# Where tiles begin in SBUF: fillers move the 256 column weight tile and the partial outputs' operands, and the branch statistics get one buffer

## The chip, the cores and the metric

The kernel runs on one core of a Trainium2 chip. The metric is the time of one execution on the device in microseconds (us), lower is better. A profiled execution and its trace come from the hardware profiler.

## The reference

One layer of a decoder trunk, sequence 2048, width 1024, all in float32:

```python
h = _rms_norm(x, pre_g)
proj = jnp.einsum('bsd,de->bse', h, w_in)            # 1024 -> 13 x 256 columns
aq, ak, av, ag, bu, bv, bg, cx, cg, dq, dk, dv, dg = jnp.split(proj, 13, axis=-1)
ya = _dilated_mixture(heads(aq), heads(ak), heads(av))   # 4 heads of 64, dilations 1, 4, 16
yb = _spatial_gating(bu, bv, sgu_g, sgu_w, sgu_b)
yc = _multiscale_pool(cx, pool_w, pool_scale)
yd = _retention(dq, dk, dv, ret_g)
y = jnp.concatenate([ya * silu(ag), yb * silu(bg), yc * silu(cg), yd * silu(dg)], axis=-1)
y = jnp.einsum('bse,ed->bsd', y, w_out)
out = x + _rms_norm(y, post_g)
```

`_dilated_mixture` runs three attention branches (dilations 4, 16, 1) per head and mixes their outputs by a softmax over their log-sum-exps.

## The kernel before, in words

**Precision.** Every large product is made of three float32r matmuls: an operand is split into a high and a low part (`hh` and `hl` for the normed input, `w[:, 0]` and `w[:, 1]` for weights, the two halves of a `yt` tile for outputs), and high times high, high times low and low times high are summed in PSUM. `mm(o, lhsT, rhs)` at L98 issues one: `lhsT` is the stationary operand, at most 128 columns, loaded into the array by a weight load (PEld) of its own; `rhs` is the moving operand, streamed through. A profile row names the output, then the moving and then the stationary operand: `ps_m<-w,hh` streams `w` through an array that holds a slice of `hh`.

**Stages.** First come the projections, in two halves of 1024 tokens. `prologue` loads x, norms it and transposes it (`ps_x`) into `hh` and `hl`. Slices of the weights are loaded and split by `weights`: 128 columns wide as `w128` or 256 wide as `w256`. Two shapes of product use them. `proj_t` (tile `ps_t`) holds 128 columns of `w128` stationary and streams 512 tokens of `hh` or `hl`. `proj_m` (tile `ps_m`) holds 128 tokens of `hh` or `hl` stationary and streams the 256 columns of `w256`; it makes `av`, `dv`, `dg` and `bv`. Results go to DRAM scratch, or feed the mixers B, C and D, which run among the projections.

Then comes attention, two pairs of heads (`attention(0)`, `attention(1)`), each head three branches: scores `ps_s`, softmax on VectorE (DVE) and ScalarE (ACT), transposes `ps_pt`, a split into `pt_hi` and `pt_lo`, and products `ps_o` with the stationary `att_v`. The first two branches of a head send their row statistics (minus the maximum, and the sum) through DRAM. The branch of dilation 1 writes its own into the third part of a tile `sv`, and `weigh` reads the others back into the first two parts and makes the mixing weights `wt`.

In the second pair's attention, nine `partial` outputs are spread: each loads a 128 token tile `yraw` of the mixers B, C and D, splits it into two `yt` tiles (`split_y`), multiplies them with `wo` (tile `ps_out`, `yt` stationary, 512 columns of `wo` moving, 36 matmuls) and stores the result `z` to `partd`. The tail, `final`, does the same for the other seven tiles, adds attention's part `ya` and `ysa`, the partial result, the norm and x (`xr`), and stores. Tile 9 of the tail takes its `yt` from the partials' buffers, the others from a pool of their own.

**Order.** A scheduler with a timeline of its own sets the order on each engine from the data dependences and the buffers; all DMAs go through SyncE's (SP) queue in its order. `tc.issue_after` ties each partial to a point of the attention.

**Places in SBUF.** Pools lie one behind the other, in order of opening, from low addresses up, and those with `side="right"` from the top down. In a pool, tiles lie in the order of their first use, a tag with n buffers taking n times its size. So a tile that is never written moves all that follow it by its size. Before, `align0` (384 bytes) and `align1` (32 twice) do that to bring the large tiles onto a multiple of 512 bytes. By these rules the tiles begin, in bytes past a multiple of 512 (before, then after where it differs):

| tile | use | before | after |
|---|---|---|---|
| `hh`, `hl` | moving in `ps_t`, stationary in `ps_m` | 0 | |
| `w128` | stationary in `ps_t` | 0 | |
| `w256` | moving in `ps_m` | 0 | 448 |
| `pt_hi`, `pt_lo` | moving in `ps_o` | 256 | |
| `att_v`, `q2`, `wo`, `ya0`, `ysa` of the tail | matmul operands | 0 | |
| `yt` of `partial` (and of tile 9) | stationary in `ps_out` | 480 | 0 |
| `yt` of the tail | stationary in `ps_out` | 0 | |
| `z`, `yraw`, `wo_raw`, `sga`, `wr`, `att_o` of the second pair | other engines, DMA, `wr` moving in `ps_f` | 480 | 0 |
| `sel` | stationary in `ps_f` | 32 | 64 |
| `sv` | statistics | 256 and 128 | 128, one place |

A slice of an operand within a tile starts at a multiple of 512 from the tile's start throughout (`w256`: 1024 bytes; a `yt` half: 512).

Of the kernel before, what the change touches and what calls it, by code (L numbers as in the profile page):

```python
# [9 lines left out]
F32 = mybir.dt.float32  # L10
# [8 lines left out]
P = 128  # L19
# [69 lines left out]
def hymba(ctx: ExitStack, tc: tile.TileContext, x, pre_g, w_in, sgu_g, sgu_w, sgu_b, pool_w,  # L89
# [4 lines left out]
    def r32(ap):  # L94
        return ap.bitcast(F32)
# [7 lines left out]
    cp = ctx.enter_context(tc.tile_pool(name="const", bufs=1))  # L103
# [15 lines left out]
    ya_d = [scratch(f"ya{g}", [P, 2, GRP]) for g in range(NG)]  # L119

    ident = cp.tile([P, P], F32, name="ident")
    cp.tile([P, 96], F32, name="align0")
    for _ in range(2):
        small.tile([P, 8], F32, tag="align1", name="align1")

# [22 lines left out]
    with ExitStack() as c1:  # L148
        k1 = c1.enter_context(tc.tile_pool(name="k1", bufs=1, side="right"))
        pa = c1.enter_context(tc.tile_pool(name="pa", bufs=1, reuse_waits="tile"))  # L150
# [40 lines left out]
        W2 = 6  # L191
        hT = {}
        first = []

        def prologue(gs, step):

# [43 lines left out]
        def weights(col, n, eng=V, scales=(1.0,)):  # L240

            if n == P:
                w = p1.tile([P, 2, KT, n], F32R, tag="w128", bufs=3, name="w128")
            else:
                w = pa.tile([P, 2, KT, n], F32R, tag="w256", bufs=1, name="w256")
            kc = KT * P // n
            for k in range(0, KT, kc):
                raw = p1.tile([P, kc, n], F32, tag="raw", bufs=2, name="raw")
                D.dma_start(raw, w_src[:, k:k + kc, col:col + n])
                for i, sc in enumerate(scales):  # L250
                    cs = slice(i * n // len(scales), (i + 1) * n // len(scales))
                    hi, lo = w[:, 0, k:k + kc, cs], w[:, 1, k:k + kc, cs]
                    A.activation(hi, raw[:, :, cs], AF.Copy, scale=sc)  # L253
                    if sc == 1.0:
                        eng.tensor_tensor(lo, raw[:, :, cs], r32(hi), ALU.subtract)  # L255
                    else:
                        V.scalar_tensor_tensor(lo, raw[:, :, cs], sc, r32(hi), ALU.mult, ALU.subtract)
            return w
# [285 lines left out]
    p3 = ctx.enter_context(tc.tile_pool(name="p3", bufs=1, side="right", reuse_waits="tile"))  # L544
# [15 lines left out]
    def attention(p, tab):  # L560
        o01 = (big if p == 0 else po).tile([P, 2, SEQ], F32, tag="big" if p == 0 else "o01", name="att_o01")
        o2 = po.tile([P, SEQ], F32, tag="o2", name="att_o2")
        o = [o01[:, 0], o01[:, 1], o2]
        wt = pc.tile([P, 3, 2, 2, 2, 8], F32, tag="wt", bufs=1, name="wt")
        for s in range(2):
            h = 2 * p + s
            rows = slice(s * HD, (s + 1) * HD)
            other = slice((1 - s) * HD, (2 - s) * HD)
            q2 = pm.tile([P, SEQ], F32R, tag="m8", bufs=7, name="q2")
            k2a = pm.tile([P, SEQ], F32R, tag="m8", bufs=7, name="k2a")  # L570
            k2b = pm.tile([P, SEQ], F32R, tag="m8", bufs=7, name="k2b")
            D.dma_start(r32(q2[rows]), qk_d[0][p][rows, 0])
            D.dma_start(r32(q2[other]), qk_d[0][p][rows, 1])
            for z in (rows, other):
                D.dma_start(r32(k2a[z]), qk_d[1][p][rows, 0])
                D.dma_start(r32(k2b[z]), qk_d[1][p][rows, 1])
            for b, dil in enumerate(DILS):
                vt = pm.tile([P, 16, 2 * HD], F32R, tag="m8", bufs=7, name="att_v")
                dst = r32(vt)
                if dil == 1:  # L580
                    src = v_d[h].rearrange("(n t c) d -> c t n d", c=4, t=32)
                    for c in range(4):
                        D.dma_start(dst[c * 32:(c + 1) * 32], src[c])
                elif dil == 4:
                    D.dma_start(dst.rearrange("q (j c) d -> q j (c d)", j=4),
                                v_d[h].rearrange("(j q c) d -> q j (c d)", j=4, c=4))
                else:
                    D.dma_start(dst.rearrange("q r d -> q (r d)"), v_d[h].rearrange("(q r) d -> q (r d)", r=16))
                qb = q2
                if dil != 1:  # L590
                    qb = pm.tile([P, SEQ], F32R, tag="m8", bufs=7, name="q2b")
                    if dil == 4:
                        src = r32(q2).rearrange("p (j k c i) -> p c j k i", j=4, c=4, i=8)
                        dst = qb.rearrange("p (j c k i) -> p c j k i", j=4, c=4, i=8)
                        for c in range(4):
                            (V if c < 3 else G).tensor_copy(dst[:, c], src[:, c])
                    else:
                        V.tensor_copy(qb.rearrange("p (r w i) -> p r w i", r=16, i=8),
                                      r32(q2).rearrange("p (w r i) -> p r w i", r=16, i=8))
                if dil == 1:  # L600
                    sv = p2.tile([P, 3, 2, 16], F32, tag="sv", bufs=2, name="sv")
                    raw = p2.tile([64, P], F32, tag="sT", bufs=1, name="sraw")
                    D.dma_start(raw, st_d[h].rearrange("b z (n q) -> (b z n) q", q=P))
                    branch(h, dil, qb, k2a, k2b, vt, tab, o[b], sv[:, b])
                    weigh(sv, raw, wt[:, :, :, s])
                    continue
                st = p2.tile([P, 2, 16], F32, tag="stat", bufs=2, name="att_st")
                branch(h, dil, qb, k2a, k2b, vt, tab, o[b], st)
                keep_stats(h, b, dil, st)
        return o01, o2, wt  # L610
# [136 lines left out]
    def weigh(sv, raw, w):  # L747

        pt = ps2.tile([P, GRP], F32, tag="t", bufs=N_T, name="ps_sv")
        transpose(pt[:, :64], raw, 64)  # L750
        V.tensor_copy(sv[:, :2].rearrange("q b z n -> q (b z n)"), pt[:, :64])
        nm = small.tile([P, 16], F32, tag="nm", name="nm")
        V.tensor_tensor(nm, sv[:, 0, 0], sv[:, 1, 0], ALU.min)
        V.tensor_tensor(nm, nm, sv[:, 2, 0], ALU.min)
        df = small.tile([P, 3, 16], F32, tag="df", name="df")
        V.tensor_tensor(df, sv[:, :, 0], nm.unsqueeze(1).broadcast_to([P, 3, 16]), ALU.subtract)
        ew = small.tile([P, 3, 16], F32, tag="ew", name="ew")
        A.activation(ew, df, AF.Exp, scale=-1.0)
        V.tensor_tensor(df, ew, sv[:, :, 1], ALU.mult)
        V.tensor_tensor(nm, df[:, 0], df[:, 1], ALU.add)  # L760
        V.tensor_tensor(nm, nm, df[:, 2], ALU.add)
        V.reciprocal(nm, nm)
        V.tensor_tensor(ew, ew, nm.unsqueeze(1).broadcast_to([P, 3, 16]), ALU.mult)
        eh = pc.tile([P, 3, 16], F32R, tag="eh", bufs=1, name="eh")
        V.tensor_copy(eh, ew)
        V.tensor_copy(w[:, :, :, 0], r32(eh).rearrange("q b (g n) -> q b g n", g=2))
        for b in range(3):
            V.tensor_tensor(w[:, b, :, 1], ew[:, b].rearrange("q (g n) -> q g n", g=2),
                            r32(eh[:, b]).rearrange("q (g n) -> q g n", g=2), ALU.subtract)
# [44 lines left out]
    def load_y(t, pool):  # L814
        raw = pool.tile([P, 6, P], F32, tag="yraw", bufs=2, name="yraw")
        D.dma_start(raw, yb_d[t // 4][:, t % 4])
        return raw

    def split_y(raw, pool, eng):

        ys = []
        for e in range(0, 6, 3):
            yt = pool.tile([P, 3, 2, P], F32R, tag="yt", bufs=2, name="yt")
            src = raw[:, e:e + 3]
            if eng is A:
                A.activation(yt[:, :, 0], src, AF.Copy)
            else:
                eng.tensor_copy(yt[:, :, 0], src)
            G.tensor_tensor(yt[:, :, 1], src, r32(yt[:, :, 0]), ALU.subtract)
            ys += [yt[:, j] for j in range(3)]  # L830
        return ys
# [12 lines left out]
    def partial(t):  # L844
        z = p3.tile([P, DM], F32, tag="z", bufs=2, name="z")
        ys = split_y(load_y(t, p3), p3, G)
        for n in range(2):
            A.activation(z[:, n * GRP:(n + 1) * GRP], out_proj(ys, range(2, 8), n, ps2, "part"), AF.Copy)
        D.dma_start(part_d[t * P:(t + 1) * P], z)
# [33 lines left out]
    with ExitStack() as c2:  # L883
        pm = c2.enter_context(tc.tile_pool(name="pm", bufs=1, reuse_waits="tile"))
        p2 = c2.enter_context(tc.tile_pool(name="p2", bufs=1, reuse_waits="tile"))
# [60 lines left out]
```

## Time and profile before

| | us |
|---|---|
| median of 3 runs | 1059.02 (1055.12 to 1059.49) |
| the profiled execution | 1055.14 |
| its span in the trace | 1053.4 |
| TensorE busy (PE) | 1000.1 |
| weight loads (PEld) | 861.6 |
| VectorE (DVE) | 519.1 |
| ScalarE (ACT) | 376.4 |
| GpSimd (POOL) | 228.0 |

Projections and mixers fill the span to about 640 us, attention 655 to 914, the tail the rest. A row of instructions gives start and length in us, engine, line, operation, tiles, shape, and how many equal ones follow each other; matmuls overlap, so a row of n lasts n - 1 steps from start to start and one full length. A row of a stretch gives the stretch, its length, and then for each engine busy time and, in brackets, how many instructions fell in it; asked for one tile, it counts that tile's instructions alone.

### The profile page before, as it was taken

Reading aid. Unit: us, or ns where it says so; the run is one execution under the profiler, and the core shown is the slowest. Engines: PE = TensorE matmul, PEld = TensorE weight load, DVE = VectorE, ACT = ScalarE, POOL = GpSimd, SP = SyncE. Lnnn points to the kernel's source line nnn. Section 1 sums busy time; section 2 is a strip of 40 time slices with the busy share of each in tenths; the row PEclk is TensorE's granted clock in tenths of the full one; section 3 lists DMA queues with packets and bytes.
Section 4 is the critical chain, followed back from the end, with each engine's and each line's share of the span. In section 5 each row is a group of like instructions: output and inputs, shape, how many; then the busy total and the mean of one; then the engine's idle time right before and its main releaser. Section 6 shows DMA issues by size and latency. Waiting matters only on the chain.

```text
span 1053.4 us, 15825 instructions
## 1 busy us (share of the span) xinstructions
PE 1000.1 (95%) x5960; PEld 861.6 (82%) x5960; DVE 519.1 (49%) x1584; ACT 376.4 (36%) x871; POOL 228.0 (22%) x217
## 2 busy tenths in 40 slices
PE   5899999999999999999999999988999989899994
PEld 5889898998888998989898888777896979776773
DVE  7621215687323331031666222176876667727776
ACT  6320313132212431031221111297873878612231
POOL 2310002221133000002120124031116411313444
PEclk9999999999999999999999999996999989989998
DMA  7530222332423232040310661187474663445565
GB/s 284 146 100 21 81 80 81 121 107 72 123 68 103 91 95 65 1 140 34 128 61 21 154 179 41 62 219 203 102 212 141 161 202 77 154 142 181 175 250 220
DMA packets 110988, 128.91 MB, mean 122 GB/s; under 512 B 9888, under 2 KB 88992, under 8 KB 108864
## 3 DMA queue, kind: packets, MB, share of 16 engines
q1 hardware_dynamic: 110912, 127.90, 39.7%
q8 instruction: 47, 0.77, 0.3%
q14 instruction: 29, 0.24, 0.1%
HBM read 91.57 MB, written 36.31 MB: 121 GB/s over the span
## 4 chain that ended last, share of the span: by engine, by line
PE 82%; DMA 7%; DVE 6%; ACT 2%; issue 2%; POOL 1%; SPq 1%; DVEq 0%; POOLq 0%; ACTq 0%
PE ps_t L98 38%; PE ps_m L98 16%; PE ps_out L98 10%; PE ps_s L98 4%; PE ps_o L98 4%; PE ps_pt L101 3%; PE ps_of L98 2%; DMA out_dram<-z 2%; DMA k2b<-qk 2%; DMA cm<-in_cmix_dram 1%; PE ps_in L98 1%; POOL z L877 1%; PE ps_mix L98 1%; DMA raw<-in_w_in_dram 1%; PE ps_x L101 1%
## 5 line engine op out<-in xcount | busy, mean ns | idle before, releaser
L98 PE MATMUL ps_t<-hh,w 128*128 128x512 f32 x1152 | 366.9, 395 | 0.0
L98 PEld LDWEIGHTS ps_t<-hh,w 128*128 128x128 f32 x1152 | 215.9, 188 | 47.8 <-issue 3.4
L98 PE MATMUL ps_t<-hl,w 128*128 128x512 f32 x576 | 226.1, 393 | 0.0
L98 PE MATMUL ps_m<-w,hh 128*128 128x256 f32 x1024 | 190.1, 286 | 1.6 <-ACT hh L235 1.6
L98 PEld LDWEIGHTS ps_m<-w,hh 128*128 128x128 f32 x1024 | 161.3, 193 | 3.3 <-ACT hh L235 2.2
L98 PE MATMUL ps_out<-wo,yt 128*128 128x512 f32 x576 | 153.9, 406 | 0.6 <-DVE z L875 0.6
L98 PE MATMUL ps_m<-w,hl 128*128 128x256 f32 x512 | 147.7, 288 | 0.1
L98 PEld LDWEIGHTS ps_t<-hl,w 128*128 128x128 f32 x576 | 108.3, 188 | 23.2 <-issue 1.4
L98 PEld LDWEIGHTS ps_out<-wo,yt 128*128 128x128 f32 x576 | 105.6, 192 | 23.1 <-issue 2.8
L255 DVE TENSOR_TENSOR w<-raw,w 128x1024 fp32r<-128x1024 f32 x42 | 58.5, 1402 | 109.5 <-ACT w L253 109.5
L98 PEld LDWEIGHTS ps_m<-w,hl 128*128 128x128 f32 x512 | 98.8, 193 | 0.8 <-DVE hl L236 0.3
L253 ACT ACTIVATE w<-raw 128x1024 fp32r<-128x1024 f32 (+1 forms) x56 | 55.0, 997 | 67.7 <-PE ps_t L98 37.3
L652 DVE CUSTOM_DVE_ANT_0 att_p<-ps_s,tab 128x128 f32<-128x128 f32 (+1 forms) x192 | 60.6, 360 | 36.3 <-PE ps_s L98 29.6
L662 DVE TENSOR_TENSOR pt_lo<-ps_pt,pt_hi 128x512 fp32r<-128x512 f32 x80 | 51.5, 652 | 18.6 <-ACT pt_hi L661 18.2
L654 ACT ACTIVATE att_p<-att_p,att_st 128x128 f32<-128x128 f32 (+1 forms) x128 | 55.0, 433 | 6.9 <-DVE att_st L652 6.4
L98 PE MATMUL ps_o<-pt_hi,att_v 128*128 128x128 f32 (+1 forms) x204 | 53.9, 284 | 1.7 <-DVE att_o L677 1.7
L98 PE MATMUL ps_o<-pt_lo,att_v 128*128 128x128 f32 (+1 forms) x204 | 52.9, 294 | 0.4 <-DVE pt_lo L662 0.4
L101 PE MATMUL ps_pt<-ident,att_p 128*128 128x128 f32 x300 | 50.6, 285 | 2.7 <-ACT att_p L654 2.5
L449 POOL TENSOR_TENSOR d_g<-d_g,ret_b 128x512 f32<-128x512 f32 x8 | 10.4, 1296 | 184.6 <-ACT d_g L447 184.6
L661 ACT ACTIVATE pt_hi<-ps_pt 128x512 fp32r<-128x512 f32 x80 | 44.1, 565 | 12.0 <-PE ps_pt L101 6.4
L98 PEld LDWEIGHTS ps_o<-pt_hi,att_v 128*128 128x128 f32 x204 | 41.0, 201 | 4.3 <-DVE att_o L677 1.9
L877 POOL TENSOR_TENSOR z<-z,xr 128x1024 f32<-128x1024 f32 x15 | 35.8, 2390 | 32.4 <-DVE z L875 27.7
(174 smaller groups left out, 1409.9 us busy)
## 6 DMA issues: line engine op xcount, KB each, us to landing
raw<-in_w_in_dram SPq DMA_DIRECT2D x52, 512.0 KB
qk<-qk_s SPq DMA_DIRECT2D x16, 512.0 KB
att_v<-vd SPq DMA_DIRECT2D x8, 1024.0 KB
xr<-in_x_dram SPq DMA_DIRECT2D x16, 512.0 KB
out_dram<-z SPq DMA_DIRECT2D x15, 512.0 KB
xt<-in_x_dram SPq DMA_DIRECT2D x7, 1024.0 KB
yraw<-yb SPq DMA_DIRECT2D x16, 384.0 KB
partd<-z SPq DMA_DIRECT2D x9, 512.0 KB
```

What stands on the lines that cost most here:

```text
L98: return T.matmul(o, lhsT, rhs, start=start, stop=stop, skip_group_check=True)
L101: T.transpose(o, i, ident[:n, :n])
L253: A.activation(hi, raw[:, :, cs], AF.Copy, scale=sc)
L255: eng.tensor_tensor(lo, raw[:, :, cs], r32(hi), ALU.subtract)
L449: G.tensor_tensor(o, o, ret_b.unsqueeze(1).broadcast_to([P, 2, 256]), ALU.mult)
L652: V.tensor_tensor_reduce(out=pr[:, u, :w], in0=ps[:, u, :w], in1=bb, scale=-SLOPES[h] * HD ** -0.5, scalar=3e38, op0=ALU.add, op1=ALU.min, ...
L654: A.activation(pr[:, u, :w], pr[:, u, :w], AF.Exp, bias=neg, scale=-1.0, accum_out=st[:, 1, n:n + 1])
L661: A.activation(hi, pt[:, :w], AF.Copy)
L662: V.tensor_tensor(lo, pt[:, :w], r32(hi), ALU.subtract)
L877: (V if last else G).tensor_tensor(z[:, ns], z[:, ns], xr[:, ns], ALU.add)
```

## The change

It adds three fillers and takes one away, and gives `sv` a single, permanent place.

- `sv` becomes `svs`, allocated once in the constants' pool where the filler `align0` stood, of the same 384 bytes; the two buffers of the tag `sv` in pool `p2` go, 768 bytes.
- In pool `pa`, ahead of the first `w256`, a filler of 448 bytes (`align2`) is laid, and behind it one of 64 (`align3`). Together 512, so all later tiles move by a whole 512.
- In pool `p3` at the top, behind the first `yt`, a filler of 480 bytes (`align4`) is laid. `p3` grows downwards, so all of `p3` and the pools opened after it on that side move 480 bytes down.

```diff
     ident = cp.tile([P, P], F32, name="ident")
-    cp.tile([P, 96], F32, name="align0")
+    svs = cp.tile([P, 3, 2, 16], F32, name="sv")
...
         first = []
+        align = []
...
             else:
+                if not align:
+                    align.append(pa.tile([P, 112], F32, name="align2"))
                 w = pa.tile([P, 2, KT, n], F32R, tag="w256", bufs=1, name="w256")
+                if len(align) == 1:
+                    align.append(pa.tile([P, 16], F32, name="align3"))
...
-                    sv = p2.tile([P, 3, 2, 16], F32, tag="sv", bufs=2, name="sv")
+                    sv = svs
...
         ys = split_y(load_y(t, p3), p3, G)
+        if t == 0:
+            p3.tile([P, 120], F32, name="align4")
```

No instruction is added or removed on any engine. The order is the same up to the last partial; in the tail the scheduler places some differently. On SP, at the end of the last partial: `ya` is attention's first pair, `partd<-z` the store of the last partial, `wo_raw` the last slice of the output weights, `xr` x for the residual, `yraw` a tile of the tail. Before:

```order
L910 DMA ya_8990<-ya_82 128x1024
L849 DMA partd<-z 128x1024
L553 DMA wo_raw<-in_w_out_dram 128x1024
L910 DMA ya_8991<-ya_83 128x1024
L911 DMA post_b<-in_post_g_dram 128x1024
L860 DMA xr<-in_x_dram 128x1024 x3
L816 DMA yraw<-yb_76 128x768
```

After:

```order
L917 DMA ya_8989<-ya_82 128x1024
L917 DMA ya_8990<-ya_83 128x1024
L918 DMA post_b<-in_post_g_dram 128x1024
L867 DMA xr<-in_x_dram 128x1024 x3
L821 DMA yraw<-yb_76 128x768
L856 DMA partd<-z 128x1024
L558 DMA wo_raw<-in_w_out_dram 128x1024
```

The store, which waits for the partial's result, and the load of `wo_raw` went behind six other loads. On PE, in the middle of the tail, where `ps_f` spreads the mixing weights of attention's second pair for VectorE and `ps_out` is the output product of the tiles. Before:

```order
L98 MATMUL ps_out<-wo_8965,ya_8990 128x512 x12
L98 MATMUL ps_f<-wr,sel 128x384 x5
L98 MATMUL ps_out<-wo_7117,yt 128x512 x6
L98 MATMUL ps_out<-wo_7126,yt 128x512 x6
L98 MATMUL ps_out<-wo_7135,yt 128x512 x6
L98 MATMUL ps_out<-wo_8965,ya_8993 128x512 x3
L98 MATMUL ps_out<-wo_8965,ysa 128x512 x3
L98 MATMUL ps_f<-wr,sel 128x384
```

After:

```order
L98 MATMUL ps_out<-wo_8964,ya_8989 128x512 x12
L98 MATMUL ps_f<-wr,sel 128x384 x6
L98 MATMUL ps_out<-wo_8964,ya_8989 128x512 x6
L98 MATMUL ps_out<-wo_8964,ysa 128x512 x12
L98 MATMUL ps_out<-wo_7117,yt 128x512 x6
L98 MATMUL ps_out<-wo_7126,yt 128x512 x5
L98 MATMUL ps_out<-wo_8964,ysa 128x512 x6
L98 MATMUL ps_out<-wo_7126,yt 128x512
```

The sixth `ps_f` no longer stands behind a whole tile of the output product, and attention's part of three partial tiles comes ahead of that tile.

## The prediction

> **What bounds the kernel now.** I read the page's busy shares and slices first, then the stretches stage by stage.
>
> ```profile
> span 1053.4 us, 15825 instructions
> PE 1000.1 (95%) x5960; PEld 861.6 (82%) x5960; DVE 519.1 (49%) x1584; ACT 376.4 (36%) x871; POOL 228.0 (22%) x217
> PEclk9999999999999999999999999996999989989998
> ```
>
> ```profile
> 0.00:50.00 50.00, 35.53 (x253) 33.07 (x254) 35.59 (x107) 26.12 (x41) 15.29 (x13) 1.00 0.69 227
> 345.00:380.00 35.00, 34.82 (x264) 33.10 (x263) 13.99 (x19) 13.97 (x21) 0.00 (x0) 1.00 0.30 91
> 450.00:640.00 190.00, 189.84 (x1190) 163.16 (x1189) 81.06 (x235) 36.73 (x50) 33.21 (x33) 1.00 0.35 103
> 680.00:760.00 80.00, 70.19 (x466) 63.19 (x466) 57.35 (x230) 68.86 (x219) 17.46 (x14) 0.89 0.67 168
> 760.00:860.00 100.00, 94.02 (x599) 81.53 (x596) 69.04 (x237) 67.34 (x202) 36.41 (x45) 0.97 0.65 186
> 960.00:1053.40 93.40, 74.97 (x320) 59.05 (x318) 66.14 (x215) 21.19 (x63) 41.79 (x23) 0.95 0.63 225
> ```
>
> The columns after each stretch's length are PE, PEld, DVE, ACT, POOL, the granted clock, the DMA share and GB/s. TensorE has no gap of note in the projection stages (189.84 of 190 us), at full clock. A nanosecond off each matmul there arrives at the end undiminished. In attention (680 to 860) PE is busy 164.2 of 180 us, 91%, and in the tail 75 of 93.4. A busy PE is not PE at its peak, so the question is how far apart matmuls start. For that I took stretches that hold one kind of matmul only, first `ps_m` (its moving operand is the 256 column weight tile), then `ps_t` (moving `hh` or `hl`, 512 columns).
>
> ```profile
> 95.00:115.00 20.00, 20.00 (x169) 20.00 (x169) 0.00 (x0) 1.79 (x3) 1.00 0.01 2
> ```
>
> ```profile
> 60.00:90.00 30.00, 30.00 (x134) 24.84 (x133) 2.08 (x3) 1.80 (x3) 1.00 0.25 71
> ```
>
> One record lasts 0.28 us in the first and 0.39 in the second, so a matmul starts each (20.00 + 0.28) / 169 = 120.0 ns and each (30.00 + 0.39) / 134 = 226.8 ns. The 256 columns more cost 106.8 ns, so streaming 256 columns takes 106.8 ns and each matmul, of either width, carries 13.2 ns beside it. All four operands of these two start on a multiple of 512 bytes. The change can win nothing but part of those 13.2 ns.
>
> **Part 1, the partial outputs' operands.** `yt` of `partial` starts 480 bytes past a multiple of 512; `yt` of most of `final` starts on one. Same instruction, same moving operand `wo`, 18 in a row, the first three rows from the partials and the last two from the tail:
>
> ```profile
> 787.74 4.36 PE L98 MATMUL ps_out<-wo,yt 128*128 128x512 f32 x18
> 801.44 4.47 PE L98 MATMUL ps_out<-wo,yt 128*128 128x512 f32 x18
> 913.92 4.42 PE L98 MATMUL ps_out<-wo,yt 128*128 128x512 f32 x18
> 993.43 4.24 PE L98 MATMUL ps_out<-wo,yt 128*128 128x512 f32 x18
> 1018.10 4.24 PE L98 MATMUL ps_out<-wo,yt 128*128 128x512 f32 x18
> ```
>
> The shift costs at least 4.36 - 4.24 = 0.12 us in 18, or 7.1 ns in each of the 17 steps; the two longer rows may hold a pause besides. The aligned rows step by (4.24 - 0.39) / 17 = 226.5 ns, as `ps_t` does. Nine partials issue 9 x 36 = 324 of these, 18 groups: 18 x 0.12 = 2.2 us. At attention's 91% that is 2.0 us, and tile 9 of the tail, which uses the same buffers, adds 2 groups or 0.2. I take -2.2 us, between 0 (if attention's waits swallow it) and 20 x 0.2 = -4.0 (if the longer rows hold no pause).
>
> The Trainium skill, "SBUF — State Buffer", section "Specifications (TRN2)", gives SBUF lines of 16 bytes, with a penalty for each cross to a new line. Both 480 and 448 are multiples of 16, so by that rule neither shift changes the lines crossed and both parts of the sum are zero, 1059.0 us. The rows above, 4.36 against 4.24 us, do not agree.
>
> **Part 2, the weight tile.** `w256` moves from a multiple of 512 to 448 past one. It is the moving operand of all `ps_m`:
>
> ```profile
> L98 PE MATMUL ps_m<-w,hh 128*128 128x256 f32 x1024 | 190.1, 286 | 1.6 <-ACT hh L235 1.6
> L98 PE MATMUL ps_m<-w,hl 128*128 128x256 f32 x512 | 147.7, 288 | 0.1
> ```
>
> That is 1536 matmuls. The same matmuls by stage:
>
> ```profile
> 0.00:50.00 50.00, 27.56 (x182) 24.37 (x182) 2.05 (x3) 1.79 (x3) 1.00 0.69 227
> 50.00:345.00 295.00, 72.72 (x586) 71.15 (x586) 0.69 (x1) 7.66 (x13) 1.00 0.28 86
> 345.00:380.00 35.00, 23.72 (x172) 21.55 (x173) 2.08 (x3) 1.79 (x3) 1.00 0.30 91
> 380.00:640.00 260.00, 73.87 (x598) 72.30 (x596) 0.69 (x1) 7.66 (x13) 1.00 0.30 88
> ```
>
> 586 + 598 = 1184 run where PE never waits and count in full. The other 352 run beside the transposes of x; from 0 to 50 PE idles 14.5 us, so I count half: 1184 + 176 = 1360.
>
> No row before has a moving operand 448 past a multiple. From below, the whole 13.2 ns beside the stream may go: -13.2 x 1360 = -18.0 us. From above, the step that `yt` pays may come to w256: +7.1 x 1360 = +9.7 us. The nearest row is the other 256 column matmul, `ps_o`, whose moving `pt_hi` and `pt_lo` start 256 past a multiple while its stationary `att_v` is on one:
>
> ```profile
> 846.63 0.28 PE L98 MATMUL ps_o<-pt_hi,att_v 128*128 128x256 f32 x1
> 846.74 0.28 PE L98 MATMUL ps_o<-pt_lo,att_v 128*128 128x256 f32 x1
> 846.86 0.28 PE L98 MATMUL ps_o<-pt_hi,att_v 128*128 128x256 f32 x1
> 846.98 0.28 PE L98 MATMUL ps_o<-pt_lo,att_v 128*128 128x256 f32 x1
> 847.10 0.28 PE L98 MATMUL ps_o<-pt_hi,att_v 128*128 128x256 f32 x1
> ```
>
> (847.10 - 846.63) / 4 = 117.5 ns: 2.5 ns better than 120.0, not worse. There is a second hint. `yt`'s 7.1 ns is about half of 13.2, as if the time beside the stream came in steps of that size, two now and three for `yt`. And the weight load shows it too:
>
> ```profile
> L98 PEld LDWEIGHTS ps_t<-hh,w 128*128 128x128 f32 x1152 | 215.9, 188 | 47.8 <-issue 3.4
> L98 PEld LDWEIGHTS ps_m<-w,hh 128*128 128x128 f32 x1024 | 161.3, 193 | 3.3 <-ACT hh L235 2.2
> ```
>
> Loads of the same size from operands that start on a multiple of 512 last 188 ns under `ps_t` and 193 under `ps_m`, so a load and a stream that start together seem to get in each other's way, and another start for the stream can end that. I take the middle between the nearest row's 2.5 ns and one step of 13.2 / 2 = 6.6: 4.5 ns, 4.5 x 1360 = -6.1 us.
>
> **Part 3, one buffer of statistics.** The next head writes `sv` only after the last read of the head before. The closest pair:
>
> ```profile
> 744.37 0.20 DVE L759 TENSOR_TENSOR df<-ew,sv 128x48 f32<-128x48 f32 x1
> 756.40 0.07 DVE L652 DVE_READ_ACCUMULATOR2_ANT sv<- 128x1 f32 x1
> ```
>
> 12 us lie between, so the new wait has ended before DVE comes to it: 0. Were this cover gone, DVE's next statistic would queue behind, and ACT's exponential waits for that.
>
> **Part 4, the tail's order.** Instructions are the same in number on every engine, and in the same order until the last partial. After that, SP issues the last partial's store and `wo_raw` behind the loads of `ya`, `post_b`, `xr` and `yraw`, and PE has six `ps_f` in one row. Nothing was measured in that order. PE's idle 18.4 us after 960 is the most a better order could win. Against it stands the longest wait there now, or the landing of `wo_raw` a few us later:
>
> ```profile
> PE ps_w L101 <- DVE wt L768: 5.4, 2, 4.2
> 1034.49 7.65 DMA out_dram<-z
> ```
>
> The tail's end is paced by stores and loads of 512 KB (the second row, from the chain, is 7.65 us of it), not by PE. I take 0, and -3 to +5 us for the range, since a single wait of the size shown is what an order typically moves.
>
> **Sum.** -2.2 - 6.1 + 0 + 0 = -8.3 us. The profiled execution took 1055.1 us (span 1053.4 and 1.7 around it) and would take 1046.8. It lies at the low end of the runs shown, whose median is 1059.0; on that median, 1050.7 us, 0.8% faster. About 0.5%, 5.3 us, is what a measurement can tell from no change.
>
> **The rivals.** First, the weight tile's place does nothing. For it: 117.5 comes from four short steps only, and 13.2 ns is the same under 256 and 512 columns, as a fixed cost of a matmul would be. Against: 193 against 188 ns for the load. Then -2.2 us, 1056.8, the same within 0.5%. The Trainium skill, "TensorE: Matmul & The Clock Gate", section "Step-by-step: what each phase is for", says the stationary and the moving operand come through two independent read ports; by that the place of one against the other is indifferent, and it is this rival's time. The trace leans against it, with 7.1 ns more where the stationary `yt` alone lies elsewhere, though `yt` may be slow by itself.
>
> Second, slower: any operand that crosses one more boundary of 512 bytes pays the `yt` step. Slices of `w256`, 1024 bytes each, touch three such stretches instead of two. Then +9.7 - 2.2 = +7.5 us, 1066.5. `ps_o` speaks against it, since `pt_hi` crosses as well and is not slower. It beats the gain of part 1 from +1.6 ns a matmul on, and is slower by 0.5% from +5.5 ns on.
>
> Third, all of the 13.2 ns goes: -18.0 - 2.2 = -20.2 us, 1038.8. No row shows a 256 column matmul at 107 ns.
>
> Fourth, the forecast holds up to 905 us and the tail's new order gives it back, +5 us: 1055.7, the same.
>
> **How the numbers follow.** Forecast 0.45 (2.5 to 6.6 ns give -5.6 to -11.2 us, 1048 to 1053.5, with the tail 1045 to 1056); nothing from the weight tile 0.27; slower by the step 0.12; all of it 0.10; lost in the tail 0.06. Faster: 0.45 + 0.10 = 0.55. Same: 0.27 + 0.06 = 0.33. Slower: 0.12. The range of 1041 to 1062 leaves out most of the third rival and of the second, near 2 in 10 together.
>
> **What would show it.** In the changed profile, a stretch of `ps_m` alone should hold about 20.28 / 0.1155 = 176 matmuls in 20 us instead of 169, and its loads should fall from 193 towards 188 ns. The partials' rows of 18 should read 4.24. `ps_t` should stay at 226.8, and the projections should end about 6 us earlier. The next write of `sv` should show no wait. I am wrong if `ps_m` stays at 120.0, if it rises towards 127, or if the attention starts earlier and the end does not.

## The result and the profile after

| | before | after |
|---|---|---|
| median, us | 1058.30 (1055.12 to 1059.49, 4 runs) | 1047.67 (1046.05 to 1048.31, 4 runs) |
| profiled execution, us | 1055.14 | 1046.05 |
| its span, us | 1053.4 | 1044.3 |

The changed kernel takes 0.9899 of the time before, 95% interval [0.9876, 0.9922]: 1.0% faster, against 0.8% forecast. In the pair of profiled executions, against which the sum was made, the gain is 9.1 us; forecast were 8.3.

The page after: span, busy time and, from its groups, the `ps_m` matmuls and their weight loads. The two numbers behind the bar are busy time in us and the mean length of one in ns.

```profile
span 1044.3 us, 15824 instructions
PE 994.1 (95%) x5960; PEld 856.4 (82%) x5960; DVE 520.7 (50%) x1584; ACT 376.7 (36%) x871; POOL 228.8 (22%) x217
L98 PE MATMUL ps_m<-w,hh 128*128 128x256 f32 x1024 | 184.8, 283 | 1.2 <-ACT hh L236 1.1
L98 PEld LDWEIGHTS ps_m<-w,hh 128*128 128x128 f32 x1024 | 158.1, 190 | 2.7 <-ACT hh L236 1.5
L98 PE MATMUL ps_m<-w,hl 128*128 128x256 f32 x512 | 145.8, 285 | 0.2 <-DVE hl L237 0.2
L98 PEld LDWEIGHTS ps_m<-w,hl 128*128 128x128 f32 x512 | 97.9, 191 | 0.8 <-DVE hl L237 0.4
```

TensorE's busy time fell by 6.0 us and that of its weight loads by 5.2; no other engine's moved by 2 us. The groups say where: `ps_m<-w,hh` lost 5.3 us, `ps_m<-w,hl` 1.9.

The stretches of the prediction again, counting `ps_m` and then `ps_t` alone. A second one of `ps_m` joins them, which held before:

```profile
141.00:161.00 20.00, 20.00 (x169) 20.00 (x169) 0.00 (x0) 1.79 (x3) 1.00 0.07 27
```

After, the two of `ps_m`, and the one of `ps_t`:

```profile
95.00:115.00 20.00, 20.00 (x172) 20.00 (x171) 0.00 (x0) 1.79 (x3) 1.00 0.00 1
141.00:161.00 20.00, 20.00 (x179) 20.00 (x178) 0.00 (x0) 1.80 (x3) 1.00 0.07 27
```

```profile
60.00:90.00 30.00, 30.00 (x134) 24.85 (x133) 2.08 (x3) 1.79 (x3) 1.00 0.24 71
```

`ps_t` holds 134 matmuls as before. `ps_m` no longer has one step: 20.28 / 172 = 117.9 ns in the first stretch and 20.28 / 179 = 113.3 in the second, where 120.0 stood in both. A step is the time from one matmul's start to the next one's. Behind the first few of a stage, single steps are 117 to 119 ns there and 113 to 114 ns, for a whole stage on end: two settled levels, not a spread.

To find where the 9.1 us lie, three points divide the span: the last `ps_t`, the start of the last partial's row of 18, and the issue of the last two loads of partial results on SP. In the timelines, before:

```profile
681.42 0.39 PE L98 MATMUL ps_t<-hh,w 128*128 128x512 f32 x1
1031.48 2.00 SPq L856 DMA_DIRECT2D z<-partd  x2
```

and after, with the partials' three rows of 18:

```profile
675.94 0.39 PE L98 MATMUL ps_t<-hh,w 128*128 128x512 f32 x1
781.61 4.27 PE L98 MATMUL ps_out<-wo,yt 128*128 128x512 f32 x18
795.21 4.37 PE L98 MATMUL ps_out<-wo,yt 128*128 128x512 f32 x18
907.67 4.32 PE L98 MATMUL ps_out<-wo,yt 128*128 128x512 f32 x18
1021.43 3.36 SPq L863 DMA_DIRECT2D z<-partd  x2
```

| stretch | before, us | after, us | difference |
|---|---|---|---|
| start to the last `ps_t` | 681.42 | 675.94 | -5.5 |
| from there to the last partial's row (before: 913.92) | 232.50 | 231.73 | -0.8 |
| from there to the last loads of `partd` | 117.56 | 113.76 | -3.8 |
| from there to the end | 21.92 | 22.87 | +0.9 |

So in this pair the projections gave 5.5 us, attention with its partials 0.8, and the tail about 2.9. The first is clear: the last `ps_t` starts at 680.6 to 682.3 us in all five traces of this study that leave `w256` on 0. The 0.8 us is not: the stretch from there to the last row takes 230.7 to 232.5 us in the five traces whose partials' `yt` stays at 480.

### The profile page after: what moved, and what is told of

Same layout as the page of the kernel before. It is cut to its first block, busy times and chain, and to the rows that moved or that the text cites. A ratio compares the mean times of both kernels' runs of the same rounds, so it can differ in the third digit from the quotient of the medians.

```text
span 1044.3 us, 15824 instructions
## 1 busy us (share of the span) xinstructions
PE 994.1 (95%) x5960; PEld 856.4 (82%) x5960; DVE 520.7 (50%) x1584; ACT 376.7 (36%) x871; POOL 228.8 (22%) x217
## 4 chain that ended last, share of the span: by engine, by line
PE 82%; DMA 8%; DVE 5%; POOL 2%; issue 1%; ACT 1%; SPq 1%; DVEq 0%; POOLq 0%; ACTq 0%
PE ps_t L98 38%; PE ps_m L98 15%; PE ps_out L98 11%; PE ps_o L98 4%; PE ps_s L98 3%; PE ps_pt L101 3%; PE ps_of L98 2%; DMA z<-partd 2%; DMA k2b<-qk 2%; DMA ret_b<-in_ret_g_dram 1%; PE ps_in L98 1%; DMA raw<-in_w_in_dram 1%; PE ps_mix L98 1%; DMA wo_raw<-in_w_out_dram 1%; DVE z L882 1%
## 5 line engine op out<-in xcount | busy, mean ns | idle before, releaser
L98 PE MATMUL ps_m<-w,hh 128*128 128x256 f32 x1024 | 184.8, 283 | 1.2 <-ACT hh L236 1.1
L98 PEld LDWEIGHTS ps_m<-w,hh 128*128 128x128 f32 x1024 | 158.1, 190 | 2.7 <-ACT hh L236 1.5
L834 POOL TENSOR_TENSOR yt<-yraw,yt 128x384 fp32r<-128x384 f32 x32 | 32.4, 1017 | 52.5 <-ACT yt L831 51.5
```

The lines of the kernel that those rows point to most:

```text
L98: return T.matmul(o, lhsT, rhs, start=start, stop=stop, skip_group_check=True)
```

## The experiments

**The weight tile alone.** The kernel before with the fillers around `w256` only:

```diff
+                if not align:
+                    align.append(pa.tile([P, 112], F32, name="align2"))
                 w = pa.tile([P, 2, KT, n], F32R, tag="w256", bufs=1, name="w256")
+                if len(align) == 1:
+                    align.append(pa.tile([P, 16], F32, name="align3"))
```

> The weight tile alone moves 448 bytes past a multiple of 512; the partials' yt stays at 480, sv keeps two buffers, and every engine has the order of the kernel before. If the shorter steps of ps_m carry the change (5.2 us less in the sum of steps of the changed trace), this run is 5 us faster than before, ratio about 0.995, with ps_m at 113 to 118 ns from start to start, rows of 18 ps_out of the partials still at 4.36 to 4.47 us, and about 13.8 us from the last matmul's start to the end. If instead most of the gain came from the tail's order and yt, it is 1 to 2 us faster at most, 0.998 to 1.000.

Measured: 1051.20 us median of 8 runs against 1058.11, ratio 0.9936 [0.9901, 0.9970], which is -6.8 us. The order on every engine is that of before. Its stretches of `ps_m` show the two levels again:

```profile
95.00:115.00 20.00, 20.00 (x172) 20.00 (x172) 0.00 (x0) 1.79 (x3) 1.00 0.01 2
141.00:161.00 20.00, 20.00 (x177) 20.00 (x178) 0.00 (x0) 1.80 (x3) 1.00 0.07 27
```

The place of `w256` by itself makes the shorter step.

**The rest of the change, in two parts.** First `svs` in the constants' pool alone, with no matmul operand moved modulo 512 (behind `sv` in `p2` lies only `ysa` of the first pair, which goes out by a DMA); then `svs` and the filler ahead of the partials' operands:

```diff
-    cp.tile([P, 96], F32, name="align0")
+    svs = cp.tile([P, 3, 2, 16], F32, name="sv")
-                    sv = p2.tile([P, 3, 2, 16], F32, tag="sv", bufs=2, name="sv")
+                    sv = svs
...
+        if t == 0:
+            p3.tile([P, 120], F32, name="align4")
```

> The single buffer sv alone; w256 at 0 and yt at 480 as before. Its order on every engine is that of the changed kernel, so this is the tail's new order without any moved operand. If the new order gives the 3 us that the changed trace gained behind its last matmul, this run is 3 us faster, ratio 0.997, with about 10.8 us from the last matmul's start to the end. If those 3 us were a chance of one execution, the ratio is 1.000 within 0.002.

> The single buffer sv and yt of the partials on a multiple of 512, w256 at 0 as before. If the shift of yt is worth what the prediction took, it is 2.2 us faster than the run with the single sv alone; if attention's waits swallow it, as the changed trace hints (0.6 to 0.8 us gained between the projections' end and the last score), it is less than 1 us faster. The partials' rows of 18 ps_out should read 4.24 in either case, and ps_m should stand at 120.0 ns.

Measured, 12 runs each: `svs` alone 1052.70 us, 0.9958 [0.9938, 0.9977]; with the filler 1052.02 us, 0.9953 [0.9932, 0.9975]. The filler's 0.7 us between the two medians cannot be told from nothing, though it does what it was to do: the last partial's row falls from 4.42 us, in the first of the two and before, to 4.32. In the first kernel:

```profile
912.91 4.42 PE L98 MATMUL ps_out<-wo,yt 128*128 128x512 f32 x18
```

In the second:

```profile
912.94 4.32 PE L98 MATMUL ps_out<-wo,yt 128*128 128x512 f32 x18
```

The gain of the two is that of `svs` alone, 0.42%. With it, both kernels have the changed kernel's order on every engine. The parts multiply to 0.9936 x 0.9953 = 0.9889, the changed kernel's 0.9899 within the intervals, so nothing is seen to be left over.

The expectations looked for this gain behind the last matmul's start, from where 13.8 us passed before and 10.8 after. It is not there: this stretch takes 12.1 us with the weight tile alone and 12.7 with `svs` alone.

**Is it the place of `sv` or the number of its buffers?** One kernel keeps `sv` in `p2` with one buffer, the other puts two permanent tiles into the constants' pool:

```diff
-                    sv = p2.tile([P, 3, 2, 16], F32, tag="sv", bufs=2, name="sv")
+                    sv = p2.tile([P, 3, 2, 16], F32, tag="sv", bufs=1, name="sv")
```

```diff
-    cp.tile([P, 96], F32, name="align0")
+    svs = [cp.tile([P, 3, 2, 16], F32, name=f"sv{i}") for i in range(2)]
+    cp.tile([P, 32], F32, name="align0")
-                    sv = p2.tile([P, 3, 2, 16], F32, tag="sv", bufs=2, name="sv")
+                    sv = svs[h % 2]
```

> The kernel before with one buffer of sv instead of two, left in its pool p2 (two runs agree that one permanent sv in the constants' pool brings 0.9958 and 0.9953). The order on every engine stays that of before. Theory one, the gain comes from the tail's new order, which the place of sv decides: ratio 1.000, tail from the last partial's first product to the end about 135.5 us as before. Theory two, the gain comes from the number of buffers: ratio 0.9955.

> The kernel before with two permanent sv tiles in the constants' pool, taken in turn by the heads; the filler behind them keeps all other tiles on their places modulo 512 bytes. The order on every engine is that of the changed kernel. Theory one (order, decided by the place): ratio 0.9955, tail about 133 to 135 us. Theory two (number of buffers): ratio 1.000.

Measured, 12 runs each: one buffer in `p2` 1.0012 [0.9986, 1.0039]; two in the constants' pool 0.9972 [0.9947, 0.9996]. The number of buffers shows no gain; the place brings one, and with it the order (the first kernel has that of before, the second that of after). The second interval ends just below 1, so its size is known poorly. In the traces both start the last partial at the same time, and part behind it. One buffer in `p2`:

```profile
911.45 4.42 PE L98 MATMUL ps_out<-wo,yt 128*128 128x512 f32 x18
1028.34 3.73 SPq L856 DMA_DIRECT2D z<-partd  x2
```

Two in the constants' pool:

```profile
911.55 4.42 PE L98 MATMUL ps_out<-wo,yt 128*128 128x512 f32 x18
1024.55 4.30 SPq L857 DMA_DIRECT2D z<-partd  x2
```

116.89 us lie between the two rows with the old order, 113.00 with the new one. Over all fourteen traces of this study the same distance is 116.9, 117.6 and 119.9 us for the three kernels with the old order, and 111.9 to 114.0 for the eleven with the new one. From the last partial's row to the end it is 139.5 to 142.3 us against 135.0 to 139.0. (The 135.5 us in the expectation count from that row's last product, 4 us later.) That the order itself, and not some other effect of the place, makes the gain is argued from this split and not isolated: no kernel had one without the other.

**Where may `w256` begin?** The same fillers with other sizes, whose sum stays 512, so that only `w256` moves. Shown for +64; the others read 64 and 64 elements (+256), 120 and 8 (+480), 32 and 96 (+128).

```diff
-                    align.append(pa.tile([P, 112], F32, name="align2"))
+                    align.append(pa.tile([P, 16], F32, name="align2"))
-                    align.append(pa.tile([P, 16], F32, name="align3"))
+                    align.append(pa.tile([P, 112], F32, name="align3"))
```

> The changed kernel with w256 64 bytes past a multiple of 512 instead of 448. If any start off the multiple helps the stream (theory one), ps_m steps at 113 to 118 ns as at 448. If the distance from the load counts, and 64 short of a boundary is the good side (theory two), 64 past is the other side and ps_m stands at 120 or above.

> The changed kernel with w256 256 bytes past a multiple of 512, as pt_hi lies. Theory one: 113 to 118 ns. Theory two, distance from the load: 117.5 as the four steps of ps_o in the trace of before, or 120 if those four steps were not yet settled. If boundaries of 256 bytes are what counts, 256 is the same as 0: 120.0.

> The changed kernel with w256 480 bytes past a multiple of 512, where yt lay. Theory one: 113 to 118. Theory two, 32 short of the boundary: between 448's 117 and 0's 120. If a start that is not a multiple of 64 is bad for a stream as well as for a load, 124 to 127.

> The changed kernel with w256 128 bytes past a multiple of 512, the middle between two multiples of 256. So far ps_m stepped at 120.0 for 0 and 256, and at 117.8 or 113.3 by stage for 64 and 448. If the distance from a multiple of 256 grows the gain, all stages step at 113.3, ps_m sums to about 185 us instead of 190, and the end comes some 4 us earlier than in the changed kernel. If any place off the multiple gives the same two levels, it is 117.8 or 113.3 by stage again and 190 us.

One run of each, so the steps are read and not the times. The two stretches of `ps_m`, at +64:

```profile
95.00:115.00 20.00, 20.00 (x172) 20.00 (x171) 0.00 (x0) 1.79 (x3) 1.00 0.00 1
141.00:161.00 20.00, 20.00 (x179) 20.00 (x179) 0.00 (x0) 1.79 (x3) 1.00 0.07 27
```

At +128:

```profile
95.00:115.00 20.00, 20.00 (x169) 20.00 (x168) 0.00 (x0) 1.80 (x3) 1.00 0.00 1
141.00:161.00 20.00, 20.00 (x171) 20.00 (x170) 0.00 (x0) 1.80 (x3) 1.00 0.07 27
```

At +256 (the second stretch holds a wait of 0.5 us):

```profile
95.00:115.00 20.00, 20.00 (x168) 20.00 (x168) 0.00 (x0) 1.79 (x3) 1.00 0.01 2
141.00:161.00 20.00, 19.50 (x162) 19.50 (x163) 0.00 (x0) 1.79 (x3) 1.00 0.07 27
```

At +480:

```profile
95.00:115.00 20.00, 20.00 (x171) 20.00 (x170) 0.00 (x0) 1.79 (x3) 1.00 0.00 1
141.00:161.00 20.00, 20.00 (x172) 20.00 (x171) 0.00 (x0) 1.80 (x3) 1.00 0.07 27
```

| `w256` at | 0 (`svs` alone) | +64 | +128 | +256 | +448 (after) | +480 |
|---|---|---|---|---|---|---|
| sum of all steps that begin with a `ps_m`, us | 194.5 | 190.3 | 193.9 | 196.0 | 189.9 | 192.5 |
| time of the one run, us | | 1046.88 | 1051.03 | 1053.50 | 1046.05 | 1047.86 |

+256 is as slow as 0: as far as these six places show, the period is 256 bytes, not 512. 64 bytes to either side of a multiple of 256 gain most, 32 short of one less. A larger gain at +128, the farthest, was expected and did not come: it keeps 120.0 in some stages and reaches 118.6 in others. +64 and +448 cannot be told apart.

**The stationary side.** The changed kernel with `w128`, the stationary operand of `ps_t`, 64 bytes off, and again with 256 bytes (64 elements for 16 in the filler):

```diff
             if n == P:
+                if len(align) == 2:
+                    align.append(p1.tile([P, 16], F32, name="align5"))
                 w = p1.tile([P, 2, KT, n], F32R, tag="w128", bufs=3, name="w128")
```

> The changed kernel, with the 128 column weight tiles (stationary in ps_t) 64 bytes past a multiple of 512 while the streams hh and hl stay on one. Theory one, that the distance between the start of the stream and the start of the weight load counts: stream minus load is then 448 modulo 512, as for ps_m in the changed kernel, and the 1728 ps_t go from 226.8 to 220 to 224.5 ns, 4 to 11 us less than the changed kernel. Theory two, that a stationary operand off the multiple is slow by itself, as yt at 480 was: ps_t goes to 233, 11 us more than the changed kernel. Theory three, that only the 256 column stream profits, since its steps are short against the load: ps_t stays at 226.8 and the time at the changed kernel's.

> The changed kernel with the stationary w128 256 bytes past a multiple of 512. At 64 past, ps_t stepped at 233.3 ns instead of 227.6 on the mean. If a load pays for each boundary of 512 that it crosses, ps_t steps at 233 here as well. If boundaries of 256 count, a load from 256 crosses one like a load from 0, and ps_t stays at 227.

Measured: +64 takes 1054.88 us, 0.9974 [0.9954, 0.9993] of before, where the changed kernel takes 0.9899: it loses 0.75%, some 8 us. `ps_t` and the two stretches of `ps_m`, at +64:

```profile
60.00:90.00 30.00, 30.00 (x131) 24.02 (x130) 2.08 (x3) 1.79 (x3) 1.00 0.24 71
```

```profile
95.00:115.00 20.00, 20.00 (x179) 20.00 (x178) 0.00 (x0) 1.80 (x3) 1.00 0.01 2
141.00:161.00 20.00, 20.00 (x178) 20.00 (x178) 0.00 (x0) 1.80 (x3) 1.00 0.07 27
```

`ps_t` at +256:

```profile
60.00:90.00 30.00, 30.00 (x134) 24.82 (x133) 1.91 (x3) 1.79 (x3) 1.00 0.24 71
```

At +64 the 30 us hold three matmuls fewer than 134; over all `ps_t` the mean step, pauses of more than 250 ns left out, rises from 227.6 to 233.3 ns and the sum of all steps from 401.9 to 411.5 us, the loss and a little more. At +256 `ps_t` does not change. The one run of it took 1050.53 us, above the changed kernel's four (1046.05 to 1048.31); where that comes from is open. Of the three theories the second fits: under 512 columns that begin on a multiple of 256, a stationary operand off one is slower. The `yt` step of the prediction (7.1 ns worse at +480) has the same sign and nearly the same size, so `yt` need not be slow by itself. Whether the place of the load counts here, or its distance from the stream, these runs do not tell, since none moves both under 512 columns.

One thing came unasked. In the +64 kernel the first stretch of `ps_m` holds 179, not 172, with `hh`, `hl` and `w256` where the changed kernel has them; only the `ps_t` ahead of it are different. But equal matmuls ahead do not fix the level either. Two later stages, `ps_m` alone, in the changed kernel:

```profile
223.00:228.00 5.00, 5.00 (x47) 5.00 (x46) 0.00 (x0) 0.60 (x1) 1.00 0.40 163
549.50:557.00 7.50, 7.50 (x66) 7.50 (x66) 0.00 (x0) 0.60 (x1) 1.00 0.00 0
```

With the weight tile alone, where all matmuls up to here are the same, in the same order and with operands at the same places modulo 512:

```profile
223.00:228.00 5.00, 5.00 (x45) 5.00 (x44) 0.00 (x0) 0.58 (x1) 1.00 0.58 203
549.50:557.00 7.50, 7.50 (x69) 7.50 (x68) 0.00 (x0) 0.60 (x1) 1.00 0.00 0
```

The first stage steps at the short level in one kernel and at the long one in the other, and the second the other way round. What picks the level of a stage is open; with one trace of each kernel, the difference in the first stretch is not shown to come from the `ps_t`.

**Streams off, loads off.** If a stream gains off the multiple and a load loses, `hh`, `hl` and `wo` 64 bytes off help `ps_t` and `ps_out`, which stream them, and hurt `ps_m`, which loads them. In the changed kernel, 64 bytes moved from ahead of `small` to the constants' pool:

```diff
-    for _ in range(2):
-        small.tile([P, 8], F32, tag="align1", name="align1")
+    cp.tile([P, 16], F32, name="align6")
```

> The changed kernel with all large tiles hh, hl and wo 64 bytes past a multiple of 512: streams of ps_t and ps_out, but loads of ps_m. Theory: a load off a multiple of 256 pays (7 ns in ps_t at 64), a stream off it gains (2 to 7 ns in ps_m). Then ps_t steps at 221 to 225 instead of 227.6 and ps_out of the tail likewise, while ps_m goes up by about 6 to 123 or 124; on the whole between 7 us faster and 4 us slower than the changed kernel. Rival: only a stream of 256 columns gains, as the load takes more of its time: ps_t stays at 227.6, ps_m pays, and the end is 10 us later.

Measured: one run, 1051.91 us. `ps_t`, then `ps_m`:

```profile
60.00:90.00 30.00, 30.00 (x133) 24.61 (x132) 2.08 (x3) 1.79 (x3) 1.00 0.24 71
```

```profile
95.00:115.00 20.00, 20.00 (x171) 20.00 (x170) 0.00 (x0) 1.80 (x3) 1.00 0.01 2
141.00:161.00 20.00, 20.00 (x170) 20.00 (x170) 0.00 (x0) 1.80 (x3) 1.00 0.07 27
```

`ps_m` loses, but not the 6 ns expected: its stages step at 118.6 or 120.0 ns (sum of steps 193.8 us). Those are the two levels of +128, and here `w256` at 448 lies 384 bytes from `hh` and `hl` at 64, which is 128 past a multiple of 256. So in every trace of this study one number describes the levels of `ps_m`: the distance between the starts of stream and load, modulo 256. Only this one run moves the load of `ps_m`, so that is a reading and not yet a rule. `ps_t` does not gain: its mean step is 229.2 ns instead of 227.6. A stream of 512 columns off the multiple is slightly slower, where one of 256 columns is faster. Each theory misses a part of this. No version here beats the changed kernel.

## Why the prediction was right

**The weight tile, -6.1 us: right in sign and size, but not by the row it was priced from.** It gave -5.5 in the trace and -6.8 alone in timed runs. The 4.5 ns were a middle between two values, the 2.5 ns that `ps_o` is better and half of the 13.2 ns, 6.6. Neither end was the answer for all: both occur, 120.0 - 117.9 = 2.1 ns in some stages and 120.0 - 113.3 = 6.7 in others. The forecast of 176 matmuls in a stretch lies between the measured 172 and 179.

But the place of `pt_hi` brings nothing: with `w256` at +256, where `pt_hi` lies, `ps_m` stays at 120.0. In the five rows of `ps_o` the whole 2.5 ns stand in the first step (846.63 to 846.74), whose matmul follows one of `ps_out`; the other three, (847.10 - 846.74) / 3, are 120 ns. So the lower value was a misread row and the upper one a guess, and that both came near a real level is luck. The reason given, that a load and a stream which start together get in each other's way, fits `ps_m`, where the distance between the two describes the step. It does not fit `ps_t`, where starting together was the fastest of the cases measured.

**The weight load as a sign: not one.** Loads were to fall from 193 towards 188 ns, and did so in part, to 190 and 191. But under `w128` at +64, where each step is 6 ns longer, the mean load of `ps_t` stays 188:

```profile
L98 PEld LDWEIGHTS ps_t<-hh,w 128*128 128x128 f32 x1152 | 215.8, 188 | 53.9 <-issue 3.4
```

There only the time from start to start shows the cost.

**The partials' operands, -2.2 us: the mechanism right, the size not.** The rows of 18 were to read 4.24 and read 4.27, 4.37 and 4.32 (4.36, 4.47 and 4.42 before): each lost 0.09 or 0.10 us, and the pauses that the longer rows were said to hold stayed. The step that failed is the one from such a row to all 18 groups and on to the end by TensorE's 91%. In the trace the 324 matmuls stand in 72 uninterrupted groups, of which three hold 18. Over the steps within these groups, pauses of more than 250 ns left out, the mean fell from 232.8 to 229.9 ns, 2.9 ns and not 7.1, which is 0.9 us in 324. How much of it arrives is not shown: the 0.8 us up to the last partial's row and the 0.7 us in timed runs both lie within the scatter. In short groups between attention's products a shorter step can end in a longer wait; that it does is argued, not isolated. The other end of the range, "if attention's waits swallow it", was the nearer one.

**One buffer of statistics, 0: right.** After, what DVE and ACT wait for ahead of the instructions on `sv` is the same three things as before (2.4, 2.7 and 0.3 us then), with nothing of the head before:

```profile
  PE ps_sv L101: 2.6, 2
  DVE sv L657: 2.3, 4
  ACT ew L763: 0.4, 1
```

One buffer in `p2`, at 1.0012, says it again.

**The tail's order, 0: too cautious.** What came with the place of `sv` is worth -0.42% as `svs` alone (4.4 us), -0.28% with two tiles (3 us), and about 2.9 us in the trace: the far end of the range of -3 to +5, or beyond it. The fear was that the store and `wo_raw` come late behind six other loads. SP's queue, before:

```profile
919.00 0.32 SPq L849 DMA_DIRECT2D partd<-z  x1
919.42 0.38 SPq L553 DMA_DIRECT2D wo_raw<-in_w_out_dram  x1
919.85 0.78 SPq L910 DMA_DIRECT2D ya<-ya  x1
920.68 0.47 SPq L911 DMA_DIRECT2D post_b<-in_post_g_dram  x1
921.19 1.81 SPq L860 DMA_DIRECT2D xr<-in_x_dram  x3
```

and after:

```profile
903.68 5.46 SPq L917 DMA_DIRECT2D ya<-ya  x4
909.18 0.43 SPq L918 DMA_DIRECT2D post_b<-in_post_g_dram  x1
909.65 1.62 SPq L867 DMA_DIRECT2D xr<-in_x_dram  x3
912.65 0.33 SPq L856 DMA_DIRECT2D partd<-z  x1
913.43 0.33 SPq L558 DMA_DIRECT2D wo_raw<-in_w_out_dram  x1
```

The store waits for the last partial's result in either order: it goes out 5.08 us after that row's start before and 4.98 after, `wo_raw` 5.50 and 5.76. The loads in front of it use time in which SP stood before a store that could not go; `xr` is issued 7.27 us after the row before and 1.98 after. Of these transfers none goes out later by more than 0.3 us. At the other end of the tail the last partial results are loaded 3.8 us earlier, and VectorE waits for them there: before

```profile
1036.66 1.30 DVE L868 TENSOR_TENSOR ps_out<-ps_out,z 128x512 f32<-128x512 f32 x2 [5.07 <-DMA z<-partd]
```

and after

```profile
1026.90 1.30 DVE L875 TENSOR_TENSOR ps_out<-ps_out,z 128x512 f32<-128x512 f32 x2 [3.43 <-DMA z<-partd]
```

Which of the moves between these two places brings the loads forward, the early `xr` or the six `ps_f` in a row, was not tried.

**The sum, -8.3 us, and luck.** Two terms missed in opposite directions: of the partials' 2.2 us less than 1 is seen, and the tail's 0 became about 3. That the total still came within a microsecond of the 9.1 us is luck.

**The rivals.** That the place of `w256` does nothing is refuted by the tile alone. It was also the time by the Trainium skill, "TensorE: Matmul & The Clock Gate", section "Step-by-step: what each phase is for", whose two independent read ports leave the place of one operand against the other indifferent. The trace doesn't agree: 64 bytes under the stationary operand alone cost 6 ns of 227.6, and 64 under a moving one of 256 columns alone gain 2 to 7 of 120. Nor does it agree with the penalty by lines of 16 bytes of the Trainium skill, "SBUF — State Buffer", section "Specifications (TRN2)", since 64, 448 and 480 are all multiples of 16. The slower rival, another boundary of 512 crossed, is refuted too: `w256` at +64 and +448 crosses one more and is faster, and at +256 it crosses one more and keeps its step. The third, all of the 13.2 ns, is reached by half (6.7).

Still open: why two levels, what picks one, why +128 gains little, and why 512 columns gain nothing. A clash between the reads of load and stream would fit that the distance counts under `ps_m`, but no run isolates it, and under 512 columns the place of the load alone fits as well.

## What to carry to other kernels

When back to back matmuls have a fixed time beside their stream, measure start to start in a stretch of one kind, compare it with a neighbour whose operands begin elsewhere, and try the place: the best here had stationary operands on a multiple of 256 bytes and a 256 column moving operand 64 bytes off one. Take such a neighbour's step from a settled row, not from the first steps behind another kind of matmul. A saving on TensorE arrived where TensorE alone sets the pace; beside attention none of it could be told from the scatter. And take an edit's effect on the order as a term of its own: ask of each transfer that moves back in a queue whether it could have gone earlier at all.

## What the runs showed of the hardware

- The step of float32r matmuls depends on where operands begin, and places 256 bytes apart gave the same step. Moving operand of 256 columns, stationary on 0: at 0 or +256, 120.0 ns; at +64 or +448, 117.9 or 113.3; at +480, 118.3; at +128, 120.0 or 118.6. With the stationary operand at 64 and the moving one at 448, 120.0 or 118.6 again, as at +128.
- Moving operand of 512 columns: 227.6 ns with both on 0 or the stationary one at +256; 233.3 with the stationary one at +64; 229.2 with the moving one at +64.
- Stages of 256 columns with the same operands settle at one of two steps, 117.9 or 113.3 ns. The stage at 223 us took the shorter in one kernel and the longer in another with the same matmuls ahead (47 and 45 in 5 us).
- The mean length of a weight load did not show a cost of 6 ns in each step: 188 ns with and without.
